# A jump of SyncE to its next block of instructions, placed ahead of the last store of a row mean

## The chip, the cores and the metric

The kernel runs on one core of a Trainium2 chip. The metric is device microseconds of one execution.

## The reference

```python
x = np.random.randn(64, 256, 8192).astype(np.float32)
def reference(x):
    return np.mean(x, axis=2)          # 16384 means over 8192 numbers each
```

It reads 536.87 MB and writes 64 KB.

## The kernel before

The 16384 rows are taken 256 at a time, two rows to each of the 128 partitions. SyncE issues every load and store; VectorE (DVE) sums; ScalarE (ACT) helps near the end. The last 128 rows come in six chunks of falling width, so that little is left to sum when the last byte has landed. Two tricks for instruction blocks and launch are already there: VectorE jumps to a fresh block before its first instruction (branch at 0.85 us, first memset at 1.46), and the first load is moved ahead of the barrier that opens the program (load at 0.00 us, the barrier's release at 0.74).

```python
FETCH_BLOCK = 128
LAST_CHUNKS = (4096, 2048, 1024, 512, 256, 256)
# ... (set-up cut)
nc.vector.addr_align(FETCH_BLOCK, offset=0, max_nops=0)   # VectorE: skip to the next multiple of 128 instructions
# ...
def store_last(r):
    nc.vector.transpose(out=fin_t[r][:], in_=fin[r][:])
    nc.sync.dma_start(out=out_last[r], in_=fin_t[r][0:P:SQ, :])
# ... 63 loads of 8 MB, each summed by one VectorE instruction (the last one half by ScalarE)
# ... the last rows: one load of 4 MB, then the six chunks, each with its own semaphore tail_sem[1..6]
scaled_sum(fin[0][:, 0:1], head[:])
store_last(0)                                              # 512 bytes, early
untracked(scaled_sum(fin[1][:, 0:1], fin_in[:, 0 : lastw + k]))._wait_ge(sem, 16)
store_last(1)                                              # 512 bytes, the last thing of all
# ... at the end of the build: the first load is moved into the head block
head_bb.instructions.insert(at, first.ins)                 # at = SyncE's drain of the head barrier
```

`addr_align(128, offset=0, max_nops=0)` asks that the next instruction of that engine stand at a multiple of 128 instructions; the padding is branched over, not run.

## Time and profile before

| kernel before | value |
|---|---|
| time, median of the 3 runs | 1247.87 us (1247.67 to 1247.88) |
| span of the profiled run | 1246.0 us |
| moved over the span | 536.96 MB at 431 GB/s |
| last chunk landed | 1242.05 us |
| from the start of the last sum to the end of the span | 3.62 us |

First the page of the kernel before: the span, its 40 slices of DMA activity in tenths, what was moved, and the queues (`q1` carries data, `q14` the engines' instructions).

```profile
span 1246.0 us, 224 instructions
...
DMA  9999999999999999999999999999999999999998
...
DMA packets 10170, 536.96 MB, mean 431 GB/s; under 512 B 1145, under 2 KB 1464, under 8 KB 1720
...
q1 hardware_dynamic: 10168, 536.94, 99.7%
q14 instruction: 2, 0.02, 0.0%
```

The queues are full until the last slice (`q1` 99.7% of the span). The kernel is bound by the stream, and two instruction packets fall within the span. Only the ends of the program can be shortened. The chain of waits that ended last, in order of time (start, length, what), for the tail of the kernel before:

```profile
1202.25 38.48 DMA xt<-in_x_dram
1240.73 0.02 issue
1240.76 1.45 DVE fin_in L95 x3
...
1242.34 0.45 DVE fin_in L101 x2
1242.79 0.02 issue
1242.82 0.21 DVE fin_t L112
```

The chain names its last computing instruction, the transpose that ends at 1243.03. The span runs 2.9 us longer: the last store and the closing barriers. The timeline has the issue of that store, and the view of the closing line (count, then duration in ns: least, median, most; first and last start) has SyncE's waits and drains after it:

```profile
1243.06 0.50 SPq L113 DMA_DIRECT2D out_dram<-fin_t  x1
```

Here are SyncE's own records in the trace, one by one, in program order (start us, duration us):

```
1243.055  0.502  issue of the last store
1243.603  0.028  wait: first store landed
1243.678  0.028  wait: second store landed
1244.608  0.028  wait: last store landed
1244.678  0.007  drain
1245.113  0.114  drain, which signals the closing barrier
1245.373  0.017  wait: barrier's release
```

From the start of the one drain to the start of the next are 0.435 us, in which SyncE does nothing else that the trace records; other neighbours stand 0.07 us apart. Last, the DMA view of the kernel before, cut to 1242 to 1247 us: 40 slices of 0.125 us, the GB/s in each, and the queues.

```profile
GB/s 0 0 0 0 0 0 0 0 0 0 0 0 0 0 0 0 0 3 1 0 0 0 0 0 0 0 0 0 0 0 66 0 0 0 0 0 0 0 0 0
...
q14 instruction: 1, 0.01, 0.4%
q1 hardware_dynamic: 8, 0.00, 0.1%
```

The 3 at 1244.2 us is the last store. The 66 at 1245.75 to 1245.88 us is one packet of instructions, 8192 bytes, starting at 1245.87, the last one in the trace's DMA records.

### The profile page before, as it was taken

How to read it: one execution, taken by the hardware profiler on the slowest of the kernel's cores; microseconds unless marked ns; L12 is line 12 of the kernel's file. 1: busy time of each engine (PE TensorE's matmuls, PEld its weight loads, DVE VectorE, ACT ScalarE, POOL GpSimd, SP SyncE). 2: the span in 40 equal slices, each digit the busy share in tenths (PEclk: the TensorE clock that was granted, in tenths of full speed). 3: DMA queues.
4: the chain of work that ended last, by engine and by line, in shares of the span. 5: the costliest groups of instructions: out<-in, count | busy, mean ns of one | idle time of the engine just before them, and what ended most of it. 6: DMA issues, size and time to landing. Idle time of an engine off the chain costs nothing.

```text
span 1246.0 us, 224 instructions
## 1 busy us (share of the span) xinstructions
PE 0.9 (0%) x2; PEld 0.4 (0%) x2; DVE 1087.3 (87%) x79; ACT 16.4 (1%) x13; POOL 0.7 (0%) x6
## 2 busy tenths in 40 slices
PE   0000000000000000000000000000000000000000
PEld 0000000000000000000000000000000000000000
DVE  2898988989889889898898988989889889898897
ACT  0000000000000000000000000000000000000004
POOL 0000000000000000000000000000000000000000
DMA  9999999999999999999999999999999999999998
GB/s 434 425 421 438 438 438 436 438 427 417 438 438 438 438 438 436 429 414 438 438 438 438 438 436 431 412 438 438 438 438 438 436 431 417 433 438 438 438 438 339
DMA packets 10170, 536.96 MB, mean 431 GB/s; under 512 B 1145, under 2 KB 1464, under 8 KB 1720
## 3 DMA queue, kind: packets, MB, share of 16 engines
q1 hardware_dynamic: 10168, 536.94, 99.7%
q14 instruction: 2, 0.02, 0.0%
HBM read 536.87 MB, written 0.07 MB: 431 GB/s over the span
## 4 chain that ended last, share of the span: by engine, by line
DMA 70%; DVE 29%; SPq 0%; issue 0%; DVEq 0%
DMA xt<-in_x_dram 70%; DVE res L95 29%; DVE fin_in L95 0%; SPq L85 0%; DVE fin_in L101 0%; DVE fin_t L112 0%; DVEq L101 0%
## 5 line engine op out<-in xcount | busy, mean ns | idle before, releaser
L95 DVE TENSOR_REDUCE res<-xt 128x2 f32<-128x16384 f32 (+1 forms) x63 | 1076.4, 17086 | 153.1 <-DMA xt<-in_x_dram 153.1
L98 ACT ACT_TABLE_LOAD x1 | 1.3, 1283 | 1181.6 <-DVE res L95 1181.6
L98 ACT ACTIVATE xt<-xt 128x8192 f32<-128x8192 f32 (+5 forms) x6 | 14.7, 2443 | 43.9 <-DMA xt<-in_x_dram 43.7
L95 DVE TENSOR_REDUCE fin_in<-xt 128x1 f32<-128x256 f32 (+3 forms) x5 | 4.9, 1005 | 0.3 <-DMA xt<-in_x_dram 0.2
L95 DVE TENSOR_REDUCE head<-xt 128x1 f32<-128x4096 f32 x1 | 4.4, 4420 | 0.2 <-DMA xt<-in_x_dram 0.2
L156 PE MATMUL ps<-ident,res 128*63 128x128 f32 x2 | 0.9, 460 | 1230.7 <-ACT xt L98 1229.6
L75 DVE MEMSET fin<- 128x32 f32 x2 | 0.1, 85 | 1.5 <-PEq L193 1.5
L98 ACT ACTIVATION_READ_ACCUMULATOR xt<-xt 128x1 f32 x6 | 1.1, 186 | 0.0
L157 DVE TENSOR_SCALAR bulk<-ps 63x128 f32<-63x128 f32 x2 | 0.6, 278 | 0.4 <-PE ps L156 0.4
L156 PEld LDWEIGHTS ps<-ident,res 128*63 128x63 f32 x2 | 0.4, 180 | 1230.9 <-issue 1229.6
L101 DVE TENSOR_SCALAR_CACHE_REDUCE fin_in<-fin_in 128x265 f32<-128x265 f32 x1 | 0.4, 430 | 0.2 <-DVE fin_in L95 0.2
L112 DVE STREAM_TRANSPOSE fin_t<-fin 128x32 f32<-128x32 f32 x2 | 0.4, 212 | 0.1
L63 POOL TENSOR_SCALAR_AFFINE_SELECT ident<-ident 128x128 f32<-128x128 f32 x1 | 0.3, 292 | 0.1
L101 DVE TENSOR_SCALAR_CACHE_REDUCE head<-head 128x2 f32<-128x2 f32 x1 | 0.2, 155 | 0.1
L62 POOL MEMSET ident<- 128x128 f32 x1 | 0.2, 204 | 0.4 <-POOLq L193 0.4
L193 POOL MEMSET const-bfloat16-1.0<- 128x1 bf16 x1 | 0.1, 101 | 0.0
L193 POOL MEMSET const-uint8-127<- 128x1 uint8 x1 | 0.1, 101 | 0.0
L193 POOL MEMSET const-float32-0.0<- 128x1 f32 x1 | 0.1, 98 | 0.2 <-issue 0.2
L193 POOL MEMSET const-float32-1.0<- 128x1 f32 x1 | 0.1, 98 | 0.0
L101 DVE DVE_READ_ACCUMULATOR head<-head 128x1 f32 x1 | 0.1, 83 | 0.0
L101 DVE DVE_READ_ACCUMULATOR fin_in<-fin_in 128x1 f32 x1 | 0.1, 83 | 0.0
## 6 DMA issues: line engine op xcount, KB each, us to landing
xt<-in_x_dram SPq DMA_DIRECT2D x1, 4096.0 KB, 31.1
xt<-in_x_dram SPq DMA_DIRECT2D x1, 2048.0 KB, 35.7
xt<-in_x_dram SPq DMA_DIRECT2D x1, 1024.0 KB, 37.7
xt<-in_x_dram SPq DMA_DIRECT2D x63, 40.8
xt<-in_x_dram SPq DMA_DIRECT2D x1, 512.0 KB, 38.5
xt<-in_x_dram SPq DMA_DIRECT2D x1, 256.0 KB, 38.7
xt<-in_x_dram SPq DMA_DIRECT2D x1, 128.0 KB, 38.5
fin_in<-in_x_dram SPq DMA_DIRECT2D x1, 128.0 KB, 38.4
```

The lines of the kernel that those rows point to most:

```text
L62: nc.gpsimd.memset(ident[:], 0.0)
L63: nc.gpsimd.affine_select(out=ident[:], in_=ident[:], compare_op=mybir.AluOpType.not_equal, fill=1.0, base=0, pattern=[[-1, P]], channel_m ...
L75: nc.vector.memset(fin[r][:], 0.0)
L95: return untracked(nc.vector.tensor_reduce(out=dst, in_=src, axis=X, op=ADD))
L98: return untracked(nc.scalar.activation(out=src, in_=src, func=COPY, accum_out=dst))
L101: return nc.vector.tensor_scalar(out=src, in0=src, scalar1=inv, scalar2=None, op0=mybir.AluOpType.mult, op1=ADD, accum_out=dst,)
L112: nc.vector.transpose(out=fin_t[r][:], in_=fin[r][:])
L156: nc.tensor.transpose(out=ps[:LB, :], in_=res[:, r, :], identity=ident[:])
L157: nc.vector.tensor_scalar_mul(out=bulk[:LB, :, r], in0=ps[:LB, :], scalar1=inv)
L193: nc = _bacc.Bacc("TRN2", target_bir_lowering=False, num_devices=1)
```

## The change

Intent, by the reading of the trace before: the pause of 0.435 us is SyncE running out of its block of instructions, and the packet at 1245.87 belongs to it. Let it go over to the next block earlier, in the 5 us in which it waits for VectorE's last sums, and at a moment when the packet that this causes meets no data.

```diff
     def store_last(r):
         nc.vector.transpose(out=fin_t[r][:], in_=fin[r][:])
-        nc.sync.dma_start(out=out_last[r], in_=fin_t[r][0:P:SQ, :])
+        return nc.sync.dma_start(out=out_last[r], in_=fin_t[r][0:P:SQ, :])
@@
     scaled_sum(fin[0][:, 0:1], head[:])
-    store_last(0)
+    st = store_last(0)
+
+    with tc.issue_after(st.ins):
+        st = nc.sync.wait_ge(tail_sem[-2], 16)
+    with tc.issue_after(st.ins):
+        st = nc.sync.addr_align(FETCH_BLOCK, offset=0, max_nops=0)
     untracked(scaled_sum(fin[1][:, 0:1], fin_in[:, 0 : lastw + k]))._wait_ge(sem, 16)
-    store_last(1)
+    with tc.issue_after(st.ins):
+        store_last(1)
```

`issue_after` fixes the order on SyncE without a wait: the trace has 83 records of SyncE before and 85 after, and the two new ones are the wait written here and the branch. `tail_sem[-2]` is the second-to-last chunk.

## The prediction

> **What bounds the kernel.** Streaming x. The page gives 536.96 MB at 431 GB/s over a 1246.0 us span. The chain that ended last is 70% DMA, 29% DVE sums. SyncE, which issues every load, waits 1178.6 us on those sums, so its issue costs the stream nothing. The change leaves loads, sums and buffers alone: about 1242 us cannot move. (The load ahead of the head barrier is in the kernel already: it is the span's first record.)
>
> **The tail.** By the chain and the trace's records, the last chunk lands at 1242.05; DVE adds it (1242.34, 0.43) and transposes (1242.82, 0.21); SyncE issues the last store at 1243.06; its landing is seen by a wait at 1244.61. Then comes a SyncE drain at 1244.68 (7 ns), and its neighbour in program order, the drain that opens the closing barrier, only at 1245.11: a gap of 0.43 us, where the same step takes 0.07 at the head and in the second closing barrier. The wait view puts 0.5 us of this on PE, but PE's drain was done at 1231.6, so I think no engine is waited for. I read it as SyncE stepping over the end of an instruction block. Two records support it: an 8192-byte instruction packet[...] at 1245.87 (DMA view of the tail), 1.2 us after the step, as the last store's packets follow its issue by 1.15; and a count: 79 SyncE instructions of the program precede the gap[...].
>
> [...] VectorE does such a jump at the head: branch at 0.85, first memset at 1.46, 0.6 us, no instruction packet in between, so its next block was resident.
>
> **What the change does.** After the first small store SyncE is idle from 1237.71 to 1243.06. Added there: one wait for the second-to-last chunk (lands 1241.75) and a jump to the next block. From VectorE's jump, 0.4 to 0.6 us (estimate): done by 1242.4, before the last store is wanted. The wait keeps the fetch that the jump starts (near 1243.0, 0.3 us long) behind the last chunk and ahead of the last store's packets. Last store, final waits and closing barriers then share a fresh block, so the gap should shrink from 0.43 to 0.07: 0.36 us, all on the critical path, since SyncE arrives last at that barrier. The time runs 1.9 us past the span; one closing hop there takes 0.16 where 0.04 is usual, near the 1245.87 packet's landing: perhaps 0.05 more.
>
> **Predicted:** 1247.87 - 0.36 - 0.05 = about 1247.45 us, range 1247.0 to 1247.9. Faster by over 2%: 0.003; within 2%: 0.99; slower by over 2%: 0.007.
>
> **What would show it.** Right: the gap between the two drains is under 0.1 us; the last instruction packet comes before 1243.5; the last store still starts 15 ns after the transpose's signal; span near 1245.6. Wrong: the gap stays at 0.43 (then it is the drain's), or the last store starts late.
>
> **What would make it wrong.** The jump's target is not resident[...]. The fetch delays the last chunk. Runs drift over 0.3 us.

What no trace or run of this case shows is cut from the recorded text where marked: an account of how instructions are fetched, sizes of an instruction block, and a time for a jump whose target must be fetched. 1247.87 - 0.36 - 0.05 = 1247.46, put as about 1247.45. The 0.36 is read from the trace (0.43 less 0.07); the 0.05 is the estimate from a hop of 0.16 us where 0.04 is usual. "Such a jump" of VectorE is its `addr_align` at the head. That the jump's target would be there and that the jump would start a packet were the estimate from VectorE's jump and the two packets of the trace before.

## More of the kernel before

```profile
L169 SPq EVENT_SEMAPHORE  x5: 17/28/28, 1243.6 to 1245.9; - x5
L169 SPq DRAIN  x3: 7/7/114, 1244.7 to 1245.5; - x3
```

Three drains, and one of them took 114 ns where the other two took 7.

## The result, and the profile after

| | before | after |
|---|---|---|
| median | 1247.80 us (1247.67 to 1248.61, 6 runs) | 1247.46 us (1247.10 to 1247.63, 6 runs) |
| last chunk landed, profiled run | 1242.05 us | 1242.44 us |
| start of last sum to end of span | 3.62 us | 3.15 us |
| span of the profiled run | 1246.0 us | 1245.9 us |

The ratio is 0.9996, 95% interval 0.9983 to 1.0009. A ratio here is the mean time of one kernel's runs over that of the other's of the same rounds, so it isn't quite the ratio of the medians quoted. The view of the closing line after the change (its number has moved from 169 to 175), and the chain's and the timeline's last lines:

```profile
L175 SPq EVENT_SEMAPHORE  x5: 17/28/28, 1244.0 to 1245.8; - x5
L175 SPq DRAIN  x3: 7/7/13, 1245.0 to 1245.4; - x3
```

```profile
1202.64 38.49 DMA xt<-in_x_dram
...
1242.71 0.45 DVE fin_in L101 x2
...
1243.18 0.21 DVE fin_t L112
```

```profile
1243.42 0.51 SPq L113 DMA_DIRECT2D out_dram<-fin_t  x1
```

No drain takes 114 ns any more. The last store still starts 0.24 us after the start of the transpose (1243.06 against 1242.82 before, 1243.42 against 1243.18 after). SyncE's records after the change:

```
1242.130  0.014  wait for the second-to-last chunk
1242.192  0.033  branch to the next block
1243.419  0.512  issue of the last store
...
1244.973  0.028  wait: last store landed
1245.038  0.013  drain
1245.108  0.007  drain, which signals the closing barrier
1245.260  0.017  wait: barrier's release
```

The two drains now stand 0.070 us apart. The DMA view over the same window, 1242 to 1247 us:

```profile
GB/s 25 25 1 0 0 0 0 0 0 66 0 0 0 0 0 0 0 0 0 0 3 1 0 0 0 0 0 0 0 0 0 0 0 0 0 0 0 0 0 0
...
q14 instruction: 1, 0.01, 0.7%
q1 hardware_dynamic: 17, 0.01, 0.5%
```

The instruction packet has gone from 1245.87 to 1243.24 us, after the last data (the 25s) and before the last store (the 3). It comes 1.05 us after the start of the branch.

The profiled spans differ by only 0.1 us, though the closing stretch is 0.477 us shorter (3.623 less 3.146). The rest is the line `DMA xt<-in_x_dram`: in this execution the stream ended 0.39 us later. Where that comes from is a question of its own, on which the later experiments bear.

### The profile page after: what moved, and what is told of

Its sections match the earlier page's. It is cut to its first block, busy times and chain, and to the rows that moved or that the text cites. A ratio compares the mean times of both kernels' runs of the same rounds, so it can differ in the third digit from the quotient of the medians.

```text
span 1245.9 us, 226 instructions
## 1 busy us (share of the span) xinstructions
PE 0.9 (0%) x2; PEld 0.4 (0%) x2; DVE 1087.3 (87%) x79; ACT 16.4 (1%) x13; POOL 0.7 (0%) x6
## 2 busy tenths in 40 slices
DMA packets 10170, 536.96 MB, mean 431 GB/s; under 512 B 1145, under 2 KB 1464, under 8 KB 1720
## 3 DMA queue, kind: packets, MB, share of 16 engines
q1 hardware_dynamic: 10168, 536.94, 99.7%
## 4 chain that ended last, share of the span: by engine, by line
DMA 70%; DVE 29%; SPq 0%; issue 0%; DVEq 0%
DMA xt<-in_x_dram 70%; DVE res L95 29%; DVE fin_in L95 0%; SPq L85 0%; DVE fin_in L101 0%; DVE fin_t L112 0%; DVEq L101 0%
```

## The experiments

"Closing stretch" is the time from the start of the last sum (line 101, 0.43 us) to the end of the span. "Trailing" is how far the last of a load's 16 landing signals lies behind the fifteenth, taken from the trace's landing records; a load gives 16 such signals, its packets run in 16 queues at once, and the kernel waits for all 16 signals. The trace gives the data packets one name, `q1`; queues are told apart by packets that follow end to start, within 0.004 us. All kernels gave correct results. `A` is the theory of the change: SyncE steps over the end of an instruction block there (a size of the block is cut from the text of the first expectation; `align256_at0` and its twin bear on it). In each set the kernel before was timed nine times in the same rounds; its medians were 1247.77, 1247.77, 1247.81 and 1247.83 us.

### One instruction more, no jump

```diff
     with tc.issue_after(st.ins):
         st = nc.sync.wait_ge(tail_sem[-2], 16)
-    with tc.issue_after(st.ins):
-        st = nc.sync.addr_align(FETCH_BLOCK, offset=0, max_nops=0)
```

> The change without its jump: SyncE has one instruction more (the wait for the second-to-last chunk) than the kernel before. Closing stretch = from the start of the last sum (L101, 0.43 us) to the end of the span: 3.62 us before, 3.15 after. Theory A[...]: the gap of 0.43 us moves one instruction earlier in program order, to between the wait for the last store's landing and the first drain; the two drains stand 0.07 apart; stretch still about 3.6; instruction packet still near the end of the span. Rival B (the gap belongs to the drain pair): gap stays between the two drains, stretch 3.6. Rival C (SyncE was only slow to wake, and the wait in between cures it): stretch 3.15. Total about 1247.8 for A and B, 1247.4 for C.

Measured: 1247.86 us (1247.74 to 1248.18, 5 runs). Closing stretch 3.65 us. SyncE's records:

```
1245.007  0.028  wait: last store landed
1245.462  0.114  drain
1245.648  0.007  drain, which signals the closing barrier
```

The pause of 0.43 us (0.455 from start to start) has moved one instruction earlier, to between the wait and the first drain, and the 114 ns have moved with it, from the second drain to the first. A drain is therefore not slow in itself: whichever of the two stands there takes the 114 ns. The pause is tied to a place in the program counted in instructions, which is A. B (the drain pair) is refuted by the place; C (the extra wait cures it) by the stretch.

### Two and five instructions more, no jump

More waits for the same chunk. The build joins them in pairs, so three written waits are two instructions, and nine are five:

```diff
     with tc.issue_after(st.ins):
-        st = nc.sync.wait_ge(tail_sem[-2], 16)
+        st = nc.sync.wait_ge(tail_sem[-2], 16)   # written 3 times in one kernel, 9 times in the other
-    with tc.issue_after(st.ins):
-        st = nc.sync.addr_align(FETCH_BLOCK, offset=0, max_nops=0)
```

> No jump, two more SyncE instructions than before (two waits for the second-to-last chunk). A: the step falls between the wait for the small first store and the wait for the last store's landing, while that store is under way (it lands 1.55 us after its issue starts), so it is hidden without any jump: stretch about 3.15, total like after (about 1247.4). B: gap stays between the drains, stretch 3.6.

> No jump, five more SyncE instructions than before. A: the step falls between the waits and the last store, while DVE adds the last chunk: stretch about 3.15, instruction packet about 1.1 us after the waits, before the last store's packets, as with the jump. B: gap stays between the drains, stretch 3.6.

Measured: with two, 1247.37 us (1247.02 to 1247.55), closing stretch 3.18, instruction packet at 1245.01. With five, 1247.36 us (1247.24 to 1247.62), closing stretch 3.16, packet at 1243.45, 1.1 us after the last of the waits. In both the drains stand 0.07 us apart. With two, the end of the block lies, by the count, between the second and third of the closing waits, and SyncE steps over it while the last store is under way; the packet at 1245.01, 1.1 us after the second of them, fits this. The pause itself can't be seen there, as SyncE would wait for the store in any case. It can be seen in `early_load_paused`, the last experiment below, which has three instructions more: there the second closing wait starts 0.481 us after the first (1243.182 and 1243.663), where the kernel before has 0.075. That wait takes 0.028 us as the others do, so a wait pays only the pause, while a drain takes 0.11 more. So the jump isn't needed for the gain; what counts is which two instructions the block's end comes between.

### The jump without its wait

```diff
-    with tc.issue_after(st.ins):
-        st = nc.sync.wait_ge(tail_sem[-2], 16)
```

> The change without its wait: SyncE jumps as soon as the first small store is issued, near 1237.7. A: gap gone as in after, and an 8192-byte instruction packet within the last chunks' stream, between about 1238.9 and 1241. At the head such a packet (VectorE's) took 0.31 us and the data packet behind it 0.53 us longer than its neighbours, so one of the 16 queues loses up to 0.8 us: if that is felt, the last chunk's last landing trails the other 15 by up to 0.8 us more than in the last chunks before it, and the total is 0 to 0.8 us over after. If the stream has room for it: last chunk on time, total like after.

Measured: 1247.38 us (1247.28 to 1247.96), closing stretch 3.14. The branch came at 1237.73, the instruction packet at 1241.22, in the middle of the last chunks. The last chunk trailed by 0.32 us, the chunk before it by 0.37: nothing was felt. In this one trace no cost of the packet is seen, so what the wait in the change is worth was not shown.

### The jump aligned to 256 instructions, twice

```diff
-        st = nc.sync.addr_align(FETCH_BLOCK, offset=0, max_nops=0)
+        st = nc.sync.addr_align(2 * FETCH_BLOCK, offset=0, max_nops=0)             # align256_at0
+        st = nc.sync.addr_align(2 * FETCH_BLOCK, offset=FETCH_BLOCK, max_nops=0)   # align256_at128
```

> The change with its jump aligned to 256 instructions, offset 0; its twin uses offset 128. One of the two must land on the next 128-block (same as the change: last store starts 15 ns after the transpose's signal, closing stretch 3.15), the other on the block after that. [...]the far one must first fetch its target: an 8192-byte instruction packet about 1.1 us after the branch, then the last store, so the store starts about 1.4 to 1.9 us after the branch, 0.2 to 0.7 us late, and the total rises to 1247.6 to 1248.1. Rival: a jump costs the same wherever it goes: both twins like the change, 1247.4.

> The twin of the run before: the same, with offset 128. Exactly one of the two is expected to be the far jump.

Measured: offset 128 is like the change, 1247.36 us (1247.11 to 1247.47, 4 runs), stretch 3.15. Offset 0 is slower than both kernels, 1248.71 us (1248.44 to 1248.74, 4 runs), stretch 4.52. The timeline of the far jump ends with:

```profile
1242.88 0.21 DVE L112 STREAM_TRANSPOSE fin_t<-fin 128x32 f32<-128x32 f32 x1
1244.34 0.53 SPq L113 DMA_DIRECT2D out_dram<-fin_t  x1
```

and its DMA view, 1242 to 1247 us, has two instruction packets:

```profile
GB/s 0 0 0 0 0 0 66 0 0 0 0 0 0 0 0 0 0 0 0 0 0 0 0 0 0 66 0 0 4 0 0 0 0 0 0 0 0 0 0 0
...
q14 instruction: 2, 0.02, 0.9%
```

The branch was at 1241.89, the first packet at 1242.79, the store at 1244.34: 2.46 us after the branch, and 1.47 us after the start of the transpose where the near jump has 0.24. The first packet started 0.90 us after the branch and 1.55 us before the store. So I read it that this jump waited for its target to be brought, and my estimate of 1.4 to 1.9 us for it was too low. The second packet, between 1245.12 and 1245.25, would be the block after the target; no run shows its contents. This is the risk that the prediction named, made real, and it fits that the change's own target was already there: its store starts 0.24 us after the start of the transpose. Of the two jumps to a multiple of 256, then, one was near (stretch 3.15) and the other far (4.52), and the instruction packets within the spans before and after, two each, have 8192 bytes. Both fit a block of 128 instructions, which is an estimate from these runs; no record counts the instructions of a packet.

### SyncE's jump at the head instead

```diff
     nc.vector.addr_align(FETCH_BLOCK, offset=0, max_nops=0)
+    nc.sync.addr_align(FETCH_BLOCK, offset=0, max_nops=0)      # in the kernel before
```

> The change itself, unaltered, in the same rounds as the run below: closing stretch (start of the last sum to the end of the span) 3.14 to 3.16 against 3.62 before, median 0.4 to 0.5 us under that of before.

> The kernel before, with SyncE's jump at the head beside VectorE's instead of in the tail. Theory A (any place where SyncE has time will do): SyncE's last instructions share one block, the drains stand 0.07 apart, no instruction packet at the end, closing stretch 3.15. Two 8192-byte instruction packets then stand in the first 10 us of the stream instead of one. If each makes its queue late, and both fall on one queue, the trailing of the last landing grows to 1 to 1.7 us and the total to 1247.8 or more; on two queues the total is 1247.4, like the change.

Measured: the change again, 1247.37 us (1247.21 to 1248.00), stretch 3.15. The jump at the head, 1247.34 us (1247.18 to 1247.53), stretch 3.14, no instruction packet at the end. Two packets stand at 6.67 and 6.78 us; the trailing over the bulk is only 0.25, because two queues are now late instead of one (the last landing lies 1.04 us behind the median of the 16). From SyncE's branch at 0.80 to its next load at 1.28 are 0.48 us, with no instruction packet before 6.67: that is what a jump to a block that is already there took, and it is hidden behind 20 us of first load. So the gain in the closing stretch needs neither the wait nor a place in the tail.

### VectorE without its own jump

The packet near 7 us is VectorE's. This run takes its cause away.

```diff
-    nc.vector.addr_align(FETCH_BLOCK, offset=0, max_nops=0)    # in the change
```

> The change without VectorE's own jump at the head. In all six traces so far one 8192-byte instruction packet stands in the first 7 us of the stream (6.6 to 7.2 us), the data packet behind it takes 2.95 us where others take 2.42, and from the first load on one of the 16 landings trails the fifteenth by 0.4 to 1.0 us, to the last chunk. Theory: that packet makes its queue late by up to 0.8 us and the whole stream waits for it. Then without it: no instruction packet near 7 us, and the trailing of the last landing in the bulk drops to 0.1 to 0.4 us. VectorE then steps over a block's end somewhere else; if that falls in its tail, its 0.5 us comes back there, so the total is open: 1247.0 to 1248.0. Rival: the late queue comes from the launch: the trailing stays at 0.4 to 1.0.

Measured: 1247.37 us (1247.27 to 1247.56), stretch 3.15. The packet now stands in the middle of the stream, at 839.03 us, where by the same reading VectorE reaches the end of its block. The DMA view of this run, 838 to 841 us, names it:

```profile
q1 hardware_dynamic: 16, 1.05, 82.1%
q14 instruction: 1, 0.01, 0.7%
```

The trailing, as a median over the loads that landed before 835 us, is 0.05; over those that landed after 845 us, 0.70. One execution, one kernel, the same queues: the packet makes its queue late, and it stays late to the end (0.64 to 0.72 in the last seven loads). The packet took 0.33 us, and the 64 KB data packet behind it took 3.08 where 2.42 is usual, so that queue lost 0.99 us. The trailing rose by less, 0.65, because this queue had not been the slowest: its data packet before that ended at 839.03, the slowest queue's at 839.30, so it was 0.27 ahead and fell 0.72 behind (by calculation); in the trace its next packet ends at 842.43, and the last of the others at 841.72, 0.71 before it. In the change the same pair is 0.31 and 2.95, a loss of 0.84. The total did not move here (1247.37, against 1247.46 and 1247.37 for the change), since the delay came back at 839 us.

### VectorE's jump earlier, in three steps

All three put VectorE's jump ahead of the head barrier, as the first load already is:

```diff
+    body_bb.instructions.remove(dve_jump.ins)
+    head_bb.instructions.insert(at, dve_jump.ins)        # at = VectorE's drain of the head barrier
```

The second also puts the first load one SyncE instruction later, behind SyncE's drain. The third puts three bare drains ahead of that, as a pause, and leaves out the jump and the wait in the tail, because three instructions more already move the block's end to a harmless place:

```diff
+    pauses = [nc.sync.drain(fusable=False) for _ in range(3)]
...
-    head_bb.instructions.insert(at, first.ins)
+    for p in pauses:
+        body_bb.instructions.remove(p.ins)
+        head_bb.instructions.insert(at, p.ins)
+    head_bb.instructions.insert(at + len(pauses) + 1, first.ins)
```

> The change with VectorE's jump moved ahead of the head barrier, as the first load is. The instruction packet then starts near 1.2 us instead of 6.6 to 7.2, where the first data packets start (1.04 to 1.8 us). If it gets in ahead of its queue's data, the trailing of the last landing drops to 0.1 to 0.5 us and the total to about 1247.0; if it falls behind the first data, it stays at 0.4 to 1.0 and the total is 1247.4, like the change.

> A try at beating both kernels: VectorE's jump ahead of the head barrier as in dve_jump_early, and the first load one SyncE instruction later, behind SyncE's own drain, so that VectorE's instruction packet may start before the data. One run (dve_no_align) showed within itself what that packet costs: the last landing trailed the fifteenth by 0.05 us before it and by 0.70 after. If the packet now starts before the data: trailing 0.05 to 0.3 us, total about 1246.9 to 1247.1. If the data still come first: packet near 4 us, trailing 0.4 to 1.0, total 1247.3 to 1247.5.

> The same with three bare drains on SyncE ahead of the load, about 0.2 us more of delay, and without the jump and the wait in the tail: three SyncE instructions more than before put the block's end between the waits of the tail, behind the last store's landing, as in two_more. Expected: closing stretch 3.15 to 3.18; VectorE's instruction packet ahead of the data, trailing 0.05 to 0.3 us, which gains 0.3 to 0.6 and costs the 0.2 to 0.3 of the pause: total 1246.9 to 1247.3. If the packet is still late: total about 1247.6.

Measured:

| kernel | first load issued | VectorE's packet | first data packet | trailing in the bulk | last chunk landed | median |
|---|---|---|---|---|---|---|
| the change | 0.00 us | 7.15 us | 1.05 us | 0.91 us | 1242.44 us | 1247.46 us |
| jump earlier | 0.00 | 4.22 | 1.03 | 0.62 | 1241.94 | 1247.18 (1247.10 to 1247.75) |
| load after the drain | 0.09 | 4.42 | 1.13 | 0.58 | 1242.12 | 1247.31 (1247.17 to 1247.39) |
| load paused | 0.24 | 1.24 | 1.28 | 0.07 | 1241.63 | 1246.90 (1246.84 to 1247.06) |

The first two are misses: the packet still came behind the first data packets, and their gain over the change is within the scatter. In the third the packet starts 0.04 us ahead of the first data, and the trailing drops to 0.07. The DMA view of the third, 0 to 3 us, shows it as one of 17 packets; for the change the same window has 16 and no `q14` line:

```profile
DMA packets 17, 1.06 MB, mean 352 GB/s; under 512 B 0, under 2 KB 0, under 8 KB 0
...
q1 hardware_dynamic: 16, 1.05, 99.9%
q14 instruction: 1, 0.01, 1.6%
```

Its tail has the gain of the change too, without the jump (closing stretch 3.14 us). All five of its runs lie below all nine runs of the kernel before in the same rounds (1247.63 to 1248.43), and below all eleven runs of the change (1247.10 to 1248.00), although those were timed in other rounds. Ratio to before 0.9992, interval 0.9980 to 1.0005. Its median is 0.9 us under the kernel before and about 0.5 under the change. The lead over the change goes with the packet's new place, but a kernel with the pause and with VectorE's jump left where it was did not run, so the pause's own share is not separated; that a packet in the stream makes its queue late is shown by `dve_no_align`.

## Why the prediction was right

The time, 1247.46 us against 1247.45, and the mechanism were right. But that the total fits to 0.01 us is luck: it was reckoned from a median of three runs, 1247.87, which is 1247.80 over six; the change's own runs lie from 1247.10 to 1247.63; and the range, 1247.0 to 1247.9, holds the kernel before as well. The gap between the drains carries the proof, not the total. Point by point:

- **Bound.** "Streaming x" held: the chain after is the same, shifted by 0.39 us, and 536.96 MB still move at 431 GB/s.
- **The pause is the end of a block.** Right, and shown by moving it: one instruction more moved it by one instruction, three put it between two waits, two or five hid it. The count in the prediction, 79 instructions, supports nothing by itself: no record shows how many the launch has.
- **0.36 us of it.** The distance between the drains fell from 0.435 to 0.070, which is 0.365. But the sum left out that the drain behind the block's end was itself slow, 0.114 against 0.007 us. Together that is 0.472 of the 0.477 us by which the closing stretch shrank. The step was mis-sized by 0.11.
- **"Perhaps 0.05 more" after the span**, the author's estimate. Wrong. The hop stands in the trace of every kernel of this study, 0.161 to 0.165 us, wherever the packet was, and the time runs 1.73 to 1.83 us past the span in all runs of the two kernels that have their span on record. The term is 0. The two errors partly cancel: 0.41 predicted, 0.48 in the closing stretch, 0.34 and 0.44 between medians in the two sets that timed the change.
- **"The wait view puts 0.5 us of this on PE".** A misreading that did no harm. SyncE's wait view after the change has the same line with the same numbers, though the pause is gone:

```profile
SPq L175 <- DMA out_dram<-fin_t: 0.9, 1, 0.9
SPq L175 <- PEq L175: 0.6, 2, 0.5
```

  The 0.6 us in two waits are the two releases of the closing barriers (by the records, 0.15 and 0.44 us). The pause appears in no view of waits; it was found by setting neighbours in program order side by side.
- **All of it on the critical path.** Right: the first barrier's release followed SyncE's drain directly before and after, 0.26 and 0.15 us from start to start, and PE, ScalarE and VectorE had signalled by 1243.09 and 1243.45, 2.1 and 1.7 us before SyncE (1245.23 and 1245.12).
- **The jump fits into the idle time.** Right. A near jump took 0.48 us in `sp_jump_at_head`, against an idle time of 1.2 us between the branch and the store. The packet came at 1243.24, not "near 1243.0".
- **"Span near 1245.6".** Missed in the profiled run (1245.9), met over the six runs (1245.3 to 1245.9). The scatter comes from the stream's end (in the two profiled runs of the change the closing stretch is 3.146 and 3.154 us, the span 1245.9 and 1245.4), and the trailing of the slowest queue is part of it: it was between 0.25 and 0.95 us across the traces that had a packet in the early stream, nearly the same from the first load to the last. Part of the 0.39 us can be followed in the two profiled traces: VectorE's packet cost its queue the same 0.84 us in both, but before the change it fell on a queue that was well ahead (its next data packet ended at 9.87 us, the last of the others at 9.58), after it on one of the slowest (10.41 and 9.68). The trailing in the bulk was 0.38 before and 0.91 after. How much else varies from run to run was not separated.

Open: why the step takes 0.43 us though no instruction packet comes during it (in the kernel before the packet starts at 1245.87, 0.75 us after the start of the drain behind the step); what the wait before the jump is worth (one trace without it showed no loss); and why VectorE's packet at the head waits as long as it does. By SyncE's 1.05 us from branch to packet, VectorE's should come near 1.9 us (an estimate: 0.85 and 1.05). In `early_load_paused`, with no data ahead of it, it did come 1.14 us after its branch (0.10 to 1.24). It came at 6.62 in the kernel before and at 7.15 in the change, each time as the second data packet of its queue ended (6.62 and 7.16), not the first (4.20 and 4.74).

## What to carry to other kernels

In a kernel whose tail is a few microseconds of one engine's bookkeeping, count that engine's instructions and look for a pause between two neighbours in program order, here 0.43 us; two or five cheap instructions earlier moved it to a place where SyncE waits anyway (closing stretch 3.18 and 3.16 us against 3.62). If a jump does it, see that it goes no further than need be: here the one aligned to 256 at offset 0 made the store 1.23 us later than the change's (1.47 and 0.24 us after the transpose). And look where the instruction packet lands: in this stream, which keeps its queues busy for 99.7% of the span, one packet of 8 KB cost its queue 0.84 to 0.99 us that were not made up by the end, and the fastest kernel here was the one where it started before the first data.
